# Attention of a hybrid decoder layer: queries' low parts by one full-height subtraction and two copies, outputs' low parts by an adding DMA, one masked product for two halves

## The chip, the cores and the metric

The kernel runs on one core of a Trainium2 chip. The metric is the device time of one execution in microseconds. Before the change the median of three runs was 1638.94 us, the runs lying between 1638.71 and 1641.65 us. The core has engines that each run their own list of instructions in order: TensorE (PE: matmuls into PSUM banks), VectorE (DVE), ScalarE (ACT), GpSimd (POOL) and SyncE (SP). GpSimd and SyncE are used here mostly to issue DMAs.

## The reference

One inference step of one layer, for a prompt of 1024 positions and 8 x 8 sample positions (1088 columns in all) with a width of 1024:

```python
xn = rmsnorm(x, norm1_g)
q, k, v, glu_a, glu_b, gate_a, gate_b = split(xn @ w_in)
# branch A: sliding-window attention, window 128, 16 query heads on 4 key/value heads, head width 64
s = q @ k.T * HEAD_DIM ** -0.5, masked to the band, one learned sink per head appended
attn = softmax(s)[..., :-1] @ v
branch_a = attn @ w_o_attn
# branch B: gated causal depthwise convolution (31 taps), LayerNorm, silu
u = glu_a * sigmoid(glu_b)
branch_b = silu(layernorm(dwconv(u))) @ w_pb
h = x + (sigmoid(gate_a) * branch_a + sigmoid(gate_b) * branch_b) @ w_out
# feed-forward with a causal depthwise convolution of 3 taps
y = h + (silu(gate) * value) @ w_down, gate and value from dwconv(rmsnorm(h) @ w_up)
```

Everything is float32; both groups get a final RMSNorm, and windows of keys, values and convolution inputs are returned too.

## The kernel before

**Products in three parts.** Each float32 operand is kept as a high part, rounded to the matmul's reduced float32 type, and a low part, which is the rest. `mm3` (L208 to L210) makes one product of three matmuls: high by high, high by low, low by high. A "stream" (`stream`, L212) takes one 1024 x 128 block of an input weight over the three chunks of columns, 384, 384 and 320 wide, with eight `mm3` each, and hands each finished PSUM bank to an evacuation routine. For most blocks of the input weight the high part is a cast on ScalarE (L179), the low part begins as its negative (ScalarE, L180), and GpSimd's DMA adds the raw weight to it (L181, `wlo<-wraw`). Raw weights come by SP (L157, `wraw<-wall`), into two buffers in turn.

**The order of the streams** is written out by hand: `b a g g g q0 q0 b a q0 q0 k0 b a v v`, `g b a g b a g g g b a`, `q1 k1 q1 q1 q1 b a g b a g g g g g g g`. Here b and a are the two halves of the gated unit of one channel block, g a gate, q0 and q1 the query blocks of the two halves of the heads, k0 and k1 their keys, v the values. After `v`, and again after the last `q1`, attention for one half (`p` = 0, then 1) is spread over the streams that follow by a count of ticks, one for each `mm3`: eight units (`attn_unit`, one for each block of 128 positions) and four sample units. A unit has for each of two key heads `g` three steps: `scores` (L440, matmuls L449 and L450), `turn` (L457, transposes and the split of the probabilities into `pth` and `ptl`), and `mix` (L476, products with the values).

**What the change touches.** `q_evac` (L815) evacuates the queries. The query tile `q0` holds for key head 0 the high part in partitions 0 to 63 and the low part in 64 to 127, and `q1` the other way round. For each chunk and each of the two tiles, ScalarE scales 64 rows into the high place (L823), and VectorE subtracts it from the bank into the low place (L824). In `turn`, two products with a band mask (L471) make the parts that belong to the block below. In `mix`, the summed result `av` is split into `q0` and `q1` at the places of the queries it came from (`split_ps`: ScalarE's cast L243, VectorE's subtraction L244). For the first half, `attn_spill` (L502) stores both parts to `d_ah` and `d_al` after blocks 3 and 7; the output projection's `o` streams load them much later (`ah`, `al`).

**The convolution** of a channel block (`conv`, L570) runs on VectorE, as some 45 multiply-adds (L582) at a low priority, so that they fill VectorE between other work. It ends with L601 to L604, and GpSimd stores the result (L605, L606, `d_c<-u`). `u` has two buffers; the next but one block's start (`u_start`, L748) loads history columns into it by SP (L752, `u<-cbT`), which must wait for that store. When all eight are stored, the LayerNorm over channels starts (`ln_steps`, L608): SP loads the results back (L634, `ct<-d_c`), VectorE adds them up (L620), and TensorE forms the mean (L628), which stands at a fixed place among the matmuls.

A scheduler fixes each engine's order of instructions when the program is built, by priorities and its own estimate of readiness; on the chip each engine then keeps to that order.

Of the kernel before, what the change touches and what calls it, by code (L numbers as in the profile page):

```python
# [6 lines left out]
F32 = mybir.dt.float32  # L7
F32R = mybir.dt.float32r
AF = mybir.ActivationFunctionType
# [120 lines left out]
class Build:  # L130
# [291 lines left out]
    def attn_unit(self, p, blk, st):  # L422
# [34 lines left out]
        def turn(g):  # L457
# [4 lines left out]
            ph = self.t(self.at, [P, 512], "pth", F32R)  # L462
            pl = self.t(self.at, [P, 512], "ptl", F32R)
            parts = [(0, ph), (0, pl)]
            with self.later(TURN_SOONER if self.now - self.gated <= 3 else 0):
                self.split_ps(ph, pl, ps)
                if blk:
                    below = self.masks[:, None, WIN:2 * WIN].to_broadcast([P, 4, WIN])
                    for x, tag in ((ph, "pth0"), (pl, "ptl0")):
                        x0 = self.t(self.at, [P, 512], tag, F32R)  # L470
                        nc.vector.tensor_tensor(x0.rearrange("p (a b) -> p a b", a=4),  # L471
                                                x.bitcast(F32).rearrange("p (a b) -> p a b", a=4), below, ALU.mult)
                        parts.append((1, x0))
            live[g]["parts"] = parts

        def mix(g):  # L476
# [6 lines left out]
            if g == 0:  # L483
                live[0]["t"] = self.t(self.at, [P, 4 * P], "av").rearrange("p (a b) -> p a b", a=4)
# [4 lines left out]
            if g == 1:  # L489
                self.split_ps(q[0][:, :, qs], q[1][:, :, qs], t)  # L490
            if p == 0 and g == 1 and blk in (3, 7):
                b0 = (blk - 3) * P
                self.attn_spill(st, slice(b0, b0 + 4 * P))
# [14 lines left out]
    def sample_unit(self, p, bp, st):  # L508
# [19 lines left out]
        def turn():  # L528
# [4 lines left out]
            ts = live["ts"] = self.t(self.at, [P, 4 * P], "av")[:, 0:2 * P]  # L533
# [196 lines left out]
    def phase_x(self):  # L730
# [60 lines left out]
        def do_a(i, u):  # L791
            self.stream(("a", i), xs, a_evac(u))
            a_done(i, u)
# [21 lines left out]
        def q_evac(p, j):  # L815
            st = q_tiles(p)

            def ev(c, o, n, ps):
                m = min(n, SEQ - o)
                for g in range(2):  # L820
                    r, x = [slice(y * HD, (y + 1) * HD) for y in (g, 1 - g)]
                    q = st["q"][g][:, j, o:o + m]
                    nc.scalar.activation(q[r], ps[r, :m], AF.Identity, scale=HD ** -0.5)  # L823
                    nc.vector.scalar_tensor_tensor(q[x], ps[r, :m], HD ** -0.5, q[r].bitcast(F32),  # L824
                                                   ALU.mult, ALU.subtract)
# [1398 lines left out]
```

## Time and profile before

| | |
|---|---|
| median of 3 runs | 1638.94 us |
| profiled execution | 1639.45 us |
| span of its instructions | 1637.7 us |
| TensorE's mean granted clock | 0.998 |
| TensorE waits named by the trace, longest first | 4.7 us (two), 2.0, 1.1, 0.6 us |

A line of a group reads: source line, engine, operation, output<-inputs, shape, number of instructions, then busy time in us and mean ns of one, then the idle time ahead of them and what ended it. A line of a timeline reads: start, duration in us, engine, line, operation, tiles, and in brackets the idle time before and what ended it; "SPq" and "POOL ... DMA" rows are the issue of a transfer, not the transfer. A line of a window reads: from and to, its length, then busy time and number of instructions on PE, PE's weight loads, DVE, ACT and POOL, the granted clock, the mean busy share of the 16 DMA engines, and GB/s. A line of DMA issues ends with the KB of one and the median us from issue to landing.

### The profile page before, as it was taken

To read this page: it belongs to the slowest core of one execution; us is meant where nothing else is said; L and a number is where in the kernel's file an instruction comes from. 1 tells how busy PE (TensorE), PEld (TensorE's weight loads), DVE (VectorE), ACT (ScalarE), POOL (GpSimd) and SP (SyncE) were. 2 spreads that over 40 slices of the span, in tenths; PEclk is the share of its full clock that TensorE was granted. 3 is DMA by queue.
4 is the path that set the end of the run, shared out by engine and by line. 5 is a ranking of instruction groups with operands and counts; after the bars stand their busy time and mean duration, and the time that the engine had idled before them with its cause. 6 is when DMAs were issued, how large, how long until landed. Compare 5 with 4: busy or idle time off the path is not lost.

```text
span 1637.7 us, 30023 instructions
## 1 busy us (share of the span) xinstructions
PE 1621.8 (99%) x11428; PEld 1602.6 (98%) x11428; DVE 1369.8 (84%) x2463; ACT 901.9 (55%) x1948; POOL 301.6 (18%) x587
## 2 busy tenths in 40 slices
PE   9999999999999999999999999999999999999998
PEld 9999999999999999999999999999999999999998
DVE  7889678999869996788755999988888877889767
ACT  6535387875588754576532465555555555524322
POOL 0210122333112221111102422322222111000000
PEclk9999999999999999999999999999999999999999
DMA  6343433545433366548763632344444334676423
GB/s 211 98 98 90 114 95 97 140 132 143 109 85 78 118 215 202 176 154 232 188 227 102 209 119 72 112 116 118 119 120 109 106 106 157 225 177 160 110 62 110
DMA packets 110329, 221.51 MB, mean 135 GB/s; under 512 B 26600, under 2 KB 57320, under 8 KB 110168
## 3 DMA queue, kind: packets, MB, share of 16 engines
q1 hardware_dynamic: 81528, 131.47, 26.0%
q0 software_dynamic: 28224, 87.71, 20.2%
q8 instruction: 90, 1.47, 0.4%
q14 instruction: 55, 0.45, 0.1%
q10 hardware_dynamic: 432, 0.40, 0.1%
HBM read 137.55 MB, written 64.03 MB: 123 GB/s over the span
## 4 chain that ended last, share of the span: by engine, by line
PE 80%; DVE 8%; DMA 4%; issue 4%; ACT 3%; POOL 0%; SPq 0%; POOLq 0%; DVEq 0%; ACTq 0%
PE mm L208 19%; PE mm L209 19%; PE mm L210 19%; PE aux L210 6%; PE aux L208 6%; PE aux L209 6%; DVE c L582 2%; PE aux L482 1%; DVE bt L582 1%; DVE q L824 1%; PE aux L461 1%; PE aux L449 1%; PE aux L450 1%; DMA ct<-d_c 1%; DMA wlo<-wraw 1%
## 5 line engine op out<-in xcount | busy, mean ns | idle before, releaser
L208 PE MATMUL mm<-xh,whi 128*128 128x384 f32 (+1 forms) x904 | 299.2, 331 | 0.2 <-ACT xh L297 0.2
L209 PE MATMUL mm<-xl,whi 128*128 128x384 f32 (+1 forms) x904 | 296.4, 328 | 0.4 <-DVE xl L298 0.4
L210 PE MATMUL mm<-xh,wlo 128*128 128x384 f32 (+1 forms) x904 | 296.3, 328 | 0.3 <-DMA wlo<-wraw 0.3
L209 PEld LDWEIGHTS mm<-xl,whi 128*128 128x128 f32 x904 | 170.5, 189 | 2.5 <-DVE xl L298 0.9
L208 PEld LDWEIGHTS mm<-xh,whi 128*128 128x128 f32 x904 | 170.5, 189 | 2.0 <-ACT xh L297 0.7
L210 PEld LDWEIGHTS mm<-xh,wlo 128*128 128x128 f32 x904 | 170.2, 188 | 1.1 <-DMA wlo<-wraw 0.7
L1470 DVE SCALAR_TENSOR_TENSOR acc<-st,fc,acc 128x1104 f32<-128x1104 f32 x88 | 119.8, 1364 | 12.2 <-issue 6.7
L582 DVE SCALAR_TENSOR_TENSOR bt<-u,consts,bt 128x513 f32<-128x513 f32 x120 | 89.6, 746 | 3.7 <-ACT bt L592 3.1
L210 PE MATMUL mm<-th,wlo 128*128 128x272 f32 x320 | 92.3, 289 | 0.0
L209 PE MATMUL mm<-tl,wlo 128*128 128x272 f32 x320 | 92.3, 288 | 0.0
L208 PE MATMUL mm<-th,wlo 128*128 128x272 f32 x320 | 92.2, 288 | 0.0
L582 DVE SCALAR_TENSOR_TENSOR c<-sm,hsum,c 128x512 f32<-128x512 f32 x120 | 89.3, 745 | 0.5
L210 PE MATMUL mm<-mh,wlo 128*128 128x272 f32 (+4 forms) x304 | 88.9, 292 | 0.0
L582 DVE SCALAR_TENSOR_TENSOR c<-u,consts,c 128x512 f32<-128x512 f32 x112 | 83.4, 744 | 0.4
L243 ACT CAST whi<-wraw 128x512 fp32r<-128x512 f32 x76 | 47.5, 625 | 62.7 <-PE aux L210 25.7
L1815 ACT COPY st<-mm 128x272 f32<-128x272 f32 (+2 forms) x132 | 43.5, 348 | 54.0 <-PE mm L210 53.8
L243 ACT CAST wlo<-wraw 128x512 fp32r<-128x512 f32 x76 | 47.3, 623 | 40.1 <-DVE wraw L1666 16.6
L1468 ACT ACTIVATE acc<-st,fc 128x1104 f32<-128x1104 f32 x44 | 57.6, 1315 | 14.9 <-DVE st L1771 11.8
L208 PE MATMUL aux<-mh,whi 128*128 128x272 f32 (+4 forms) x216 | 63.8, 295 | 0.0
L209 PE MATMUL aux<-ml,whi 128*128 128x272 f32 (+4 forms) x216 | 63.5, 294 | 0.0
L244 DVE TENSOR_TENSOR wlo<-wraw,wlo 128x512 fp32r<-128x512 f32 x76 | 52.7, 695 | 9.5 <-ACT wlo L243 9.3
L208 PEld LDWEIGHTS mm<-th,wlo 128*128 128x128 f32 x320 | 60.2, 188 | 0.0
(726 smaller groups left out, 5799.2 us busy)
## 6 DMA issues: line engine op xcount, KB each, us to landing
wraw<-wall SPq DMA_DIRECT2D x118, 512.0 KB, 3.8
wlo<-wraw POOLq DMA_DIRECT2D x37, 512.0 KB, 4.5
bw<-d_b SPq DMA_DIRECT2D x42, 272.0 KB, 3.9
d_b<-gd POOLq DMA_DIRECT2D x36, 272.0 KB, 6.1
d_b<-acc POOLq DMA_DIRECT2D x24, 272.0 KB, 4.7
ar<-wdn SPq DMA_DIRECT2D x32, 192.0 KB, 3.8
d_g<-acc POOLq DMA_DIRECT2D x10, 544.0 KB, 4.7
ga<-d_ga SPq DMA_DIRECT2D x8, 544.0 KB, 5.4
```

Of the source, the lines that this page charges most:

```text
L208: mm(ps, wh, xh, start=first, stop=False, skip_group_check=more)
L209: mm(ps, wh, xl, start=False, stop=False, skip_group_check=more)
L210: self.last_mm = mm(ps, wl, xh, start=False, stop=last, skip_group_check=more).ins
L243: self.cast = self.nc.scalar.copy(h, src).ins
L244: self.low = self.nc.vector.tensor_tensor(l, src, h.bitcast(F32), ALU.subtract).ins
L449: nc.tensor.matmul(ps[:, j, :], q[g][:, h, qs], kd[g][:, keys], start=True, stop=False)
L450: nc.tensor.matmul(ps[:, j, :], q[g][:, h, qs], kl[g][:, keys], start=False, stop=True)
L461: nc.tensor.transpose(ps[:, h * P:(h + 1) * P], pt[:, h, 0:P], self.ident)
L582: mac = lambda o, x, w: nc.vector.scalar_tensor_tensor(o, x, w, o, ALU.mult, ALU.add)
L1468: nc.scalar.activation(acc, st[:, 0:AW], AF.Identity, bias=fb(f), scale=fw(f, 0))
L1470: nc.vector.scalar_tensor_tensor(acc, st[:, k:k + AW], fw(f, k), acc, ALU.mult, ALU.add)
L1815: self.evicted = (add if second and n == 0 and j == 1 else op)(d, r(banks[bank, j]))
```

## The change

`q_evac` scales all 128 rows into `q0` (ScalarE), subtracts all 128 rows into a new tile `ql` with two buffers (VectorE, one instruction), scales 64 rows into `q1`, and SP copies the two halves of `ql` to their places. `turn` keeps the two parts in one tile and masks them with one product of 1024 columns. `mix` has two buffers for `av`; the low part of the output begins as the negative of the high part (ScalarE) and GpSimd's DMA adds `av` to it. The first spill moves from block 3 to block 4, and `do_a` asks for one more split weight where a value stream comes next.

```diff
@@ turn
-            ph = self.t(self.at, [P, 512], "pth", F32R)
-            pl = self.t(self.at, [P, 512], "ptl", F32R)
-            parts = [(0, ph), (0, pl)]
+            x = self.t(self.at, [P, 2, 512], "pt", F32R)
+            parts = [(0, x[:, y]) for y in range(2)]
...
-                    below = self.masks[:, None, WIN:2 * WIN].to_broadcast([P, 4, WIN])
-                    for x, tag in ((ph, "pth0"), (pl, "ptl0")):
-                        x0 = self.t(self.at, [P, 512], tag, F32R)
-                        nc.vector.tensor_tensor(x0.rearrange("p (a b) -> p a b", a=4),
-                                                x.bitcast(F32).rearrange("p (a b) -> p a b", a=4), below, ALU.mult)
-                        parts.append((1, x0))
+                    below = self.masks[:, None, WIN:2 * WIN].to_broadcast([P, 8, WIN])
+                    x0 = self.t(self.at, [P, 2, 512], "pt0", F32R)
+                    nc.vector.tensor_tensor(x0.rearrange("p y (a b) -> p (y a) b", a=4),
+                                            x.bitcast(F32).rearrange("p y (a b) -> p (y a) b", a=4), below, ALU.mult)
+                    parts += [(1, x0[:, y]) for y in range(2)]
@@ mix
-                live[0]["t"] = self.t(self.at, [P, 4 * P], "av").rearrange("p (a b) -> p a b", a=4)
+                live[0]["t"] = self.t(self.at, [P, 4 * P], "av", bufs=2).rearrange("p (a b) -> p a b", a=4)
...
-                self.split_ps(q[0][:, :, qs], q[1][:, :, qs], t)
-            if p == 0 and g == 1 and blk in (3, 7):
-                b0 = (blk - 3) * P
+                h, l = q[0][:, :, qs], q[1][:, :, qs]
+                nc.scalar.copy(h, t)
+                nc.scalar.activation(l, h.bitcast(F32), AF.Identity, scale=-1.0)
+                nc.gpsimd.dma_start(l, t, accum_op=ALU.add)
+            if p == 0 and g == 1 and blk in (4, 7):
+                b0 = blk // 7 * 4 * P
@@ do_a
-            self.stream(("a", i), xs, a_evac(u))
+            self.stream(("a", i), xs, a_evac(u), ahead=1 + (self.order[self.w_used + 1][0] == "v"))
@@ q_evac
-                for g in range(2):
-                    r, x = [slice(y * HD, (y + 1) * HD) for y in (g, 1 - g)]
-                    q = st["q"][g][:, j, o:o + m]
-                    nc.scalar.activation(q[r], ps[r, :m], AF.Identity, scale=HD ** -0.5)
-                    nc.vector.scalar_tensor_tensor(q[x], ps[r, :m], HD ** -0.5, q[r].bitcast(F32),
-                                                   ALU.mult, ALU.subtract)
+                q0, q1 = [q[:, j, o:o + m] for q in st["q"]]
+                low = self.t(self.at, [P, 384], "ql", F32R, bufs=2)[:, :m]
+                nc.scalar.activation(q0, ps[:, :m], AF.Identity, scale=HD ** -0.5)
+                nc.vector.scalar_tensor_tensor(low, ps[:, :m], HD ** -0.5, q0.bitcast(F32), ALU.mult,
+                                               ALU.subtract)
+                nc.scalar.activation(q1[HD:], ps[HD:, :m], AF.Identity, scale=HD ** -0.5)
+                nc.sync.dma_start(q0[HD:].bitcast(F32), low[:HD].bitcast(F32))
+                nc.sync.dma_start(q1[:HD].bitcast(F32), low[HD:].bitcast(F32))
```

Lines behind these places carry numbers that are one to three higher in the changed kernel.

The change moves instructions at three places that matter below. The first is VectorE at the last chunks of the last `q1` stream, ahead of the first scores of the second half. The `c`, `bt` and `u` rows are a convolution and its end. Before:

```order
L824 SCALAR_TENSOR_TENSOR q_508_4287<-mm_4702,q_508_4287 64x384
L582 SCALAR_TENSOR_TENSOR c_4226<-sm_4227,hsum_87,c_4226 128x512
L824 SCALAR_TENSOR_TENSOR q_509_4288<-mm_4702,q_509_4288 64x384
L601 TENSOR_SCALAR u_3956<-c_4226,consts_77 128x64
L602 TENSOR_TENSOR c_4226<-c_4226,bt_4228 128x512
L604 TENSOR_TENSOR u_3956<-c_4226,bt_4228 128x512
L603 TENSOR_TENSOR u_3956<-c_4226 128x512
L824 SCALAR_TENSOR_TENSOR q_508_4287<-mm_4731,q_508_4287 64x384
L824 SCALAR_TENSOR_TENSOR q_509_4288<-mm_4731,q_509_4288 64x384
L824 SCALAR_TENSOR_TENSOR q_508_4287<-mm_4760,q_508_4287 64x256
L824 SCALAR_TENSOR_TENSOR q_509_4288<-mm_4760,q_509_4288 64x256
```

Now:

```order
L583 SCALAR_TENSOR_TENSOR c_4214<-sm_4215,hsum_87,c_4214 128x512
L602 TENSOR_SCALAR u_3949<-c_4214,consts_77 128x64
L603 TENSOR_TENSOR c_4214<-c_4214,bt_4216 128x512
L605 TENSOR_TENSOR u_3949<-c_4214,bt_4216 128x512
L824 SCALAR_TENSOR_TENSOR ql_4662<-mm_4637,q_490_4275 128x384
L604 TENSOR_TENSOR u_3949<-c_4214 128x512
L824 SCALAR_TENSOR_TENSOR ql_4693<-mm_4668,q_490_4275 128x256
L824 SCALAR_TENSOR_TENSOR ql_4733<-mm_4708,q_490_4275 128x384
L824 SCALAR_TENSOR_TENSOR ql_4764<-mm_4739,q_490_4275 128x384
L824 SCALAR_TENSOR_TENSOR ql_4795<-mm_4770,q_490_4275 128x256
```

The convolution's end stood behind the first chunk of the last query block (two subtractions); now it stands behind the middle chunk of the block before it, four subtractions of the old kind sooner, and one subtraction to `ql` takes the place of two.

The second is SP's queue at the same place, which had no query copies; before it read:

```order
L157 DMA wraw_541_4695<-wall 128x1024
L157 DMA wraw_548_4795<-wall 128x1024
L752 DMA u_643_5426<-cbT 128x8x30
L157 DMA wraw_568_4951<-wall 128x1024
L157 DMA wraw_613_5237<-wall 128x1024
```

Now, with the copies of the last two query blocks:

```order
L827 DMA q0_490_4275<-ql_529_4662 64x384
L828 DMA q1_491_4276<-ql_529_4662 64x384
L827 DMA q0_490_4275<-ql_531_4693 64x256
L828 DMA q1_491_4276<-ql_531_4693 64x256
L753 DMA u_629_5429<-cbT 128x8x30
L827 DMA q0_490_4275<-ql_536_4733 64x384
L828 DMA q1_491_4276<-ql_536_4733 64x384
L157 DMA wraw_542_4807<-wall 128x1024
L827 DMA q0_490_4275<-ql_538_4764 64x384
L828 DMA q1_491_4276<-ql_538_4764 64x384
L827 DMA q0_490_4275<-ql_540_4795 64x256
L828 DMA q1_491_4276<-ql_540_4795 64x256
```

The history load `u<-cbT`, which waits for the convolution's store, stood among weight loads; now six copies of the last query block stand behind it.

The third is GpSimd's queue at the last block of the first half's attention: the spill (`d_ah`, `d_al`; eight issues, of which the first row here is the seventh) and a weight's adding DMA (`wlo`). Before:

```order
L505 DMA d_ah_1_57<-q0_27_123 128x512
L506 DMA d_al_2_58<-q1_28_124 128x512
L517 DMA vp_603_5132<-vp 128x2x128
L393 COPY sp_605_5140<-nsrow_19_88 128x1
L181 DMA wlo1_500_4125<-wraw_471_3960 128x1024
```

Now, with the adding DMA of the last block's output, `q1<-av`, among them:

```order
L813 MEMSET qs_492_4277 128x768
L393 COPY sp_593_5145<-nsrow_19_88 128x1
L506 DMA d_ah_1_57<-q0_27_123 128x512
L491 DMA q1_28_124<-av_468_4004 128x4x128
L506 DMA d_ah_1_57<-q0_27_123 128x512 x3
L507 DMA d_al_2_58<-q1_28_124 128x512 x4
L181 DMA wlo1_482_4113<-wraw_457_3953 128x1024
```

The load of `vp` now stands behind the weight's adding DMA and the small copy `sp` ahead of the spill; the adding DMA of the output stands inside the spill, whose later rows read what it writes, and all of it ahead of the weight's.

More of the change, by code (lines that the diff above doesn't have):

```diff
@@ L532, in turn @@
             nc.tensor.transpose(tr[:, P:2 * P], pt[:, 0, 64:192], self.ident)
-            ts = live["ts"] = self.t(self.at, [P, 4 * P], "av")[:, 0:2 * P]
+            ts = live["ts"] = self.t(self.at, [P, 4 * P], "av", bufs=2)[:, 0:2 * P]
             nc.scalar.copy(ts, tr[:, 0:2 * P])
```

2 lines of the change are left out of this document (1 added, 1 removed).

## The prediction

> **What bounds the kernel now.** I read the page's busy line first, then TensorE's waits (us in total, times, longest), then TensorE's timeline and windows around each.
>
> ```profile
> PE 1621.8 (99%) x11428; PEld 1602.6 (98%) x11428; DVE 1369.8 (84%) x2463; ACT 901.9 (55%) x1948; POOL 301.6 (18%) x587
> PE aux L628 <- DVE sm L620: 4.7, 2, 3.4
> PE mm L209 <- DMA wlo<-wraw: 2.0, 1, 2.0
> PE mm L714 <- DVE least L708: 1.1, 1, 1.1
> ```
>
> TensorE is busy for 1621.8 of 1637.7 us. The change removes none of its matmuls, so all it can win is TensorE's idle time, some 16 us by the busy line, and what a halved clock costs after an idle stretch. Nearly all that the waits name lies in four places: 4.7 us in two waits of the LayerNorm mean (L628), 2.0 us for one low weight part, 0.58 us at an attention score (next fence), and 1.1 us at L714, which is at the start of the program and untouched. So the question is not how much VectorE saves in all, but what stands behind three of these waits. The places:
>
> ```profile
> 177.99 0.28 PE L208 MATMUL mm<-whi,xh 128*128 128x256 f32 x1
> 180.31 0.39 PE L209 MATMUL mm<-wlo,xh 128*128 128x256 f32 x1 [2.04 <-DMA wlo<-wraw]
> ...
> 460.37 0.39 PE L449 MATMUL aux<-kd,q 128*128 128x256 f32 x1 [0.58 <-DVE ptl L244]
> ...
> 629.05 1.24 PE L628 MATMUL aux<-sm,mean 128*128 128x272 f32 x2 [3.36 <-DVE sm L620]
> ...
> 692.90 0.72 PE L628 MATMUL aux<-sm,mean 128*128 128x272 f32 x2 [1.37 <-DVE sm L620]
> ```
>
> The third costs more than its 3.36 us:
>
> ```profile
> 628.00:630.00 2.00, 0.95 (x3) 0.84 (x3) 1.49 (x4) 0.48 (x1) 0.75 (x2) 0.76 1.15 345
> 630.00:632.00 2.00, 2.00 (x9) 1.91 (x8) 1.42 (x4) 0.00 (x0) 0.17 (x1) 0.50 0.94 373
> 632.00:634.00 2.00, 2.00 (x14) 2.00 (x14) 2.00 (x1) 0.00 (x0) 0.00 (x0) 0.88 0.05 20
> ```
>
> The third column from the end is the granted clock: 0.76, 0.50, 0.88. The shares lost, 0.24, 0.50 and 0.12 of 2 us each, make 1.7 us. The wait of 2.04 us left the clock at 1.00 (its window, 175 to 200 us, shows 1.00). A page of the Trainium skill, "TensorE: Matmul & The Clock Gate", says under "Part 1: The HAM clock gate" that the clock halves after about one idle window of 3.4 us. The trace agrees at this one place: 3.36 us idle, then half speed; by that rule any shorter wait left here would give back the 1.7 us as well.
>
> **The change part by part.** First the prices on VectorE, ScalarE and the queues.
>
> ```profile
> L824 DVE SCALAR_TENSOR_TENSOR q<-mm,q 64x384 fp32r<-64x384 f32 x32 | 17.8, 555 | 1.6 <-ACT q L823 0.6
> L824 DVE SCALAR_TENSOR_TENSOR q<-mm,q 64x256 fp32r<-64x256 f32 x16 | 6.8, 422 | 2.3 <-ACT q L823 1.9
> L244 DVE TENSOR_TENSOR aw<-ar,aw 128x384 fp32r<-128x384 f32 x24 | 13.3, 554 | 2.0 <-ACT aw L243 1.4
> L471 DVE TENSOR_TENSOR ptl<-ptl,masks 128x512 fp32r<-128x512 f32 x28 | 19.1, 683 | 0.0
> L1480 DVE TENSOR_TENSOR acc<-acc,acc 128x1024 f32<-128x1024 f32 x22 | 26.8, 1217 | 0.0
> L244 DVE TENSOR_TENSOR q<-av,q 128x512 fp32r<-128x512 f32 x16 | 11.0, 686 | 1.9 <-ACT q L243 1.8
> L243 ACT CAST q<-av 128x512 fp32r<-128x512 f32 x16 | 9.8, 613 | 1.0 <-DVE av L488 1.0
> L180 ACT ACTIVATE wlo<-whi 128x1024 fp32r<-128x1024 f32 x37 | 39.1, 1057 | 0.2
> wlo<-wraw POOLq DMA_DIRECT2D x37, 512.0 KB, 4.5
> d_c<-u POOLq DMA_DIRECT2D x8, 512.0 KB, 2.9
> d_ga<-gt POOLq DMA_DIRECT2D x16, 192.0 KB, 2.2
> ```
>
> - Queries: a 128x384 subtraction takes 554 ns and a 64x384 one 555, so rows are free. 48 subtractions become 24: VectorE saves 16 x 0.555 + 8 x 0.422 = 12.3 us. ScalarE keeps its number of instructions. SP issues 48 more copies of up to 96 KB. No row shows such a copy. Its landing is bounded below by 0 and above by the 2.2 us of a 192 KB store; I take 2.2, the nearest row.
> - Masks: 56 products of 0.683 become 28 of 1024 columns. The nearest row, L1480, has 1217 ns, so VectorE saves 28 x (1.366 - 1.217) = 4.2 us.
> - Attention outputs: 16 subtractions of 0.686 go, 11.0 us of VectorE. ScalarE gets 16 more activations of 512 columns; the bounds are 0.613 (the cast of that size) and 1.057 (L180, twice as wide), I take 0.613, so 9.8 us. GpSimd gets 16 adding DMAs of 256 KB, which should land in 2.2 to 4.5 us by the 192 KB and 512 KB rows; I take the middle, 3.4. Their result is read only by a spill to memory and by the output projection, far later.
>
> Together VectorE loses some 27 us of its 1369.8. What is it worth at each place?
>
> **Place A, 180 us.** The low weight part that TensorE waits for comes out of a long chain in order on ScalarE, behind the evacuation of the first keys.
>
> ```profile
> 123.68 0.55 DVE L824 SCALAR_TENSOR_TENSOR q<-mm,q 64x384 fp32r<-64x384 f32 x1
> ...
> 147.31 0.43 DVE L824 SCALAR_TENSOR_TENSOR q<-mm,q 64x256 fp32r<-64x256 f32 x1
> ...
> 155.74 0.47 ACT L849 CAST kd<-mm 64x384 fp32r<-64x384 f32 x1 [1.18 <-DVE kl L848]
> 157.24 1.05 ACT L179 CAST whi<-wraw 128x1024 fp32r<-128x1024 f32 x1
> 169.24 1.05 ACT L179 CAST p<-wraw 128x1024 fp32r<-128x1024 f32 x1 [5.29 <-DMA wraw<-wall]
> 175.08 0.87 POOL L181 DMA_DIRECT2D wlo<-wraw  x1 [2.35 <-ACT wlo L180]
> ```
>
> Read backwards: the adding DMA at 175.08 follows casts that waited for a raw load (169.24), which waited for the slot of the weight cast at 157.24, which stood behind a key copy that waited for VectorE's L848. VectorE worked without a break there. Between 123.68 and 147.31 it ran 12 of the query subtractions, 8 wide and 4 narrow. Six of them go: 4 x 0.555 + 2 x 0.422 = 3.1 us. The chain moves up by as much, the DMA to 172.0, its landing from 180.3 to about 177.2, and it is wanted 0.15 us after 177.99. The wait goes: **-2.0 us**. Bounds: 0 if the keys then wait for TensorE instead, -2.04 in full.
>
> **Place B, 460 us.** ScalarE and VectorE alternate on the chunks of the last query group until the row below, though TensorE began the scores of the second half at 440.50 (quoted further down); from there ScalarE has no gap up to the cast that leads to the score at 460.37.
>
> ```profile
> 445.70 0.42 DVE L824 SCALAR_TENSOR_TENSOR q<-mm,q 64x256 fp32r<-64x256 f32 x1 [0.94 <-ACT q L823]
> ```
>
> A shorter evacuation brings all of it forward: **-0.6**. Bounds: 0 and -0.6, and the new cost below.
>
> **Place C, 629 us.** This is the largest piece. It starts at the end of the last convolution.
>
> ```profile
> 612.94 0.68 DVE L603 TENSOR_TENSOR u<-c 128x512 f32<-128x512 f32 x1
> 613.92 0.54 POOL L605 DMA_DIRECT2D d_c<-u  x1 [1.26 <-DVE u L603]
> 616.75 0.33 SPq L157 DMA_DIRECT2D wraw<-wall  x1
> 620.37 2.28 SPq L634 DMA_DIRECT2D ct<-d_c  x3
> 475.00:600.00 125.00, 125.00 (x792) 120.91 (x791) 121.65 (x238) 97.76 (x278) 26.91 (x48) 1.00 0.40 109
> 608.00:620.00 12.00, 12.00 (x75) 12.00 (x74) 5.62 (x10) 2.88 (x3) 2.51 (x4) 1.00 1.04 368
> 620.00:622.00 2.00, 2.00 (x13) 2.00 (x12) 0.00 (x0) 1.93 (x3) 0.16 (x1) 1.00 0.25 67
> ```
>
> VectorE is full from 475 to 600 us (121.65 of 125), with the second half's attention ahead of the convolutions. There it saves 8 x 0.686 for the outputs and 14 x 0.149 for the masks, 7.6 us, so the convolution ends near 606 instead of 613.6. But TensorE will not get 7.6 us: the reload of the result (L634) stands on SP behind a weight load issued at 616.75, so it can rise from 620.37 to about 617.1 at most. And the DMA engines are full until 620 (share 1.04) and slack only from 620 to 622 (0.25): 1.5 us of work fits there. So the reload ends between 1.5 and 3.3 us earlier. I take 2.2, nearer to the bandwidth's end. The wait shrinks from 3.36 to 1.2: **-2.2**, and with a wait of 1.2 us, below the 2.04 that left the clock alone, the halved clock goes: **-1.7**.
>
> The fourth place (692.90) hangs on TensorE's own progress, so I leave it: 0, bounds -1.4 and +1.5 (the size of that wait, either way).
>
> **New costs.** ScalarE's activations add 8 x 0.613 = 4.9 us to the 97.76 of 125 us between 475 and 600, where TensorE does not wait at all now; the spare time covers them, and if it didn't, TensorE would wait for as much. On SP a new hazard stands ahead of the first scores of the second half.
>
> ```profile
> 441.05 0.68 DVE L603 TENSOR_TENSOR u<-c 128x512 f32<-128x512 f32 x1
> ...
> 445.16 0.55 SPq L752 DMA_DIRECT2D u<-cbT  x1
> ...
> 440.50 0.28 PE L449 MATMUL aux<-kd,q 128*128 128x256 f32 x1
> ```
>
> The copies of the last query group stand behind the history load (u<-cbT), which waits until the previous convolution has been stored. That convolution ended at 441.73. Four query subtractions that ran ahead of its end now stand behind it (2 x 0.555 + 2 x 0.422 = 2.0 us), and the eight chunks before it have one subtraction instead of two (8 x 0.51 = 4.1 us): it ends at 435.6 at the latest, and up to 7.6 us sooner if what VectorE saves in the first half's attention (8 x 0.686 + 14 x 0.149) carries over. From its end to the copies' landing I count 0.54 (issue of the store) + 2.9 + 0.55 + 2 x 0.4 + 2.2 = 7.0 us. That gives 435.0 to 442.6, against 440.50: TensorE waits for between 0 and 2.1 us. The middle, 438.8, is in time; I take **+0.5** for the later part of that stretch.
>
> On GpSimd the adding DMA of the first half's last block, and the spill that reads it, stand ahead of a weight's adding DMA; the spill must wait for the landing taken above, so that weight can come between 0 and 3.4 us later. Against that, two small steps that it stood behind now stand elsewhere, and the spill's eight DMAs stood ahead of it before too. I take 0 and keep 3.4 as an end. The first spill comes one block later and no longer reads a fresh result; its reader is the output projection, much later: 0. A second buffer for the outputs can only take waits away: 0. The edit of `do_a` has a weight split asked for one stream sooner ahead of the first value stream; on ScalarE the two casts of place A keep their order, so 0, bounds 0 and the 2.0 us of A.
>
> A rule speaks against these copies: "DMA: Bandwidth & Descriptors" in the Trainium skill, under "Rules for kernel authors", advises against two transfers to disjoint partition halves, because they serialize. No run here shows such a pair; by it the second copy lands one transfer later, at most another 2.2 us in the estimate above.
>
> **The sum:** -2.0 - 0.6 - 2.2 - 1.7 + 0.5 = -6.0 us against the profiled 1639.45 us, so 1633.45. The median, 1638.94, is 0.5 us below the profiled execution; I give the same step from there: **1633 us**. With every term at its favourable end (C -3.3, fourth place -1.4, no new wait) it is -9.0, 1630.
>
> **The rivals.**
> - *The wait at 629 stays.* The reload is bound by the DMA engines and by SP's order, not by VectorE; a residue of some 3 us keeps the half clock. For it: the share of 1.04 until 620. Against it: the 1.5 us of slack after it. Then only A and B and the +0.5 count: -2.1, so about 1636.8, within 0.2%.
> - *Nothing is won.* VectorE's time is filled with convolution anyway, and the key evacuation at 155 us is set by TensorE. Then about 1639. Against it: VectorE is without a gap ahead of both places.
> - *A new wait outweighs all.* The history load on SP blocks the copies. If the convolution ended as late as now, 441.7, the copies would land at 448.7 and TensorE would stand still for 8.2 us at 440.5, with 1.7 us of half clock behind it: +9.9, against A, C and the clock's -5.9 a net +4, 1643. It decides from a convolution end of about 433.5, and the whole is slower by more than 0.2% if it ends after 441.
> - *More is won*: the wait at 629 goes in full and the one at 693 with it, 1630.
>
> **How the numbers follow.** Forecast with its terms within a microsecond or two: 0.60. Wait at 629 stays: 0.17. Nothing won: 0.08. New wait outweighs: 0.10. More won: 0.05. A measurement of this kernel tells some 0.2%, 3.3 us, from no change, so faster begins below 1635.7. The forecast's upper edge, with the full wait of 2.1 us at 440 (1634.6), is still faster; 0.03 of its chance, with two terms short at once, is not. So faster 0.57 + 0.05 = 0.62, same 0.03 + 0.17 + 0.07 = 0.27, slower 0.10 + 0.01 = 0.11. The range, from 1629.5 to 1638, leaves out the slower rival and most of the one without a gain.
>
> **What would show it.** Right: no wait of L209 for wlo<-wraw near 178; none of L449 for ptl near 458; L628's first wait near 623 below 2 us, with a granted clock of 1.00 behind it; the last d_c<-u issued some 7 us earlier against TensorE's work; no new row in TensorE's waits above 1 us. Wrong: a wait of L449 for DMA q<-ql near 438; L628 still waiting for over 3 us with 0.50 behind it; waits for ScalarE between 470 and 600; VectorE's busy time down by much less than 27 us.

## The result and the profile after

The changed kernel takes 1645.17 us (median of 7 runs, 1643.63 to 1646.45), the kernel before 1638.94 beside it (7 runs): ratio 1.0034, with a 95% interval from 1.0022 to 1.0046. It is **slower by about 0.34%**. The forecast was 1633 us with a range up to 1638.0, so the time lies outside it, on the other side of no change. The profiled execution of the changed kernel is the fastest of the seven, 1643.63 us, with a span of 1641.9 against 1637.7. The two traces below differ by 4.2 us; by the ratio the medians differ by some 5.6, and no trace shows the rest.

The first fence has the busy line of the changed kernel's page; the second its TensorE waits (total, times, longest, in us).

```profile
PE 1624.3 (99%) x11428; PEld 1604.0 (98%) x11428; DVE 1344.5 (82%) x2395; ACT 912.2 (56%) x1964; POOL 329.0 (20%) x603
```

```profile
PE aux L629 <- DVE sm L621: 6.0, 2, 4.7
PE mm L210 <- DMA wlo<-wraw: 1.8, 1, 1.8
PE mm L209 <- DMA wlo<-wraw: 1.3, 1, 1.3
```

VectorE lost 1369.8 - 1344.5 = 25.3 us of work, as meant. TensorE nevertheless waits longer: the mean (L629, formerly L628) waited 4.7 us in all and now 6.0, and a wait of 1.8 us for a weight is new. The score's wait is gone, and that for the first weight has shrunk from 2.0 to 1.3. Where that happens is read by following the same instruction in both traces. TensorE's timeline, changed kernel:

```profile
179.50 0.39 PE L209 MATMUL mm<-wlo,xh 128*128 128x256 f32 x1 [1.27 <-DMA wlo<-wraw]
...
382.17 0.34 PE L209 MATMUL mm<-xl,whi 128*128 128x384 f32 x1
384.33 0.51 PE L210 MATMUL mm<-xh,wlo 128*128 128x384 f32 x1 [1.82 <-DMA wlo<-wraw]
...
444.92 0.28 PE L449 MATMUL aux<-kd,q 128*128 128x256 f32 x1
...
629.29 0.34 PE L210 MATMUL mm<-xh,wlo 128*128 128x384 f32 x1
634.35 1.25 PE L629 MATMUL aux<-sm,mean 128*128 128x272 f32 x2 [4.72 <-DVE sm L621]
...
697.92 0.73 PE L629 MATMUL aux<-sm,mean 128*128 128x272 f32 x2 [1.32 <-DVE sm L621]
```

And those of the same instructions in the kernel before that were not shown above:

```profile
381.37 0.34 PE L209 MATMUL mm<-xl,whi 128*128 128x384 f32 x1
381.55 0.35 PE L210 MATMUL mm<-xh,wlo 128*128 128x384 f32 x1
...
625.35 0.34 PE L210 MATMUL mm<-xh,wlo 128*128 128x384 f32 x1
```

| TensorE's instruction | before | after | later by |
|---|---|---|---|
| behind the first weight's wait | 180.31 | 179.50 | -0.8 |
| in front of the new wait | 381.37 | 382.17 | +0.8 |
| behind the new wait | 381.55 | 384.33 | +2.8 |
| first scores of the second half | 440.50 | 444.92 | +4.4 |
| in front of the mean | 625.35 | 629.29 | +3.9 |
| the mean | 629.05 | 634.35 | +5.3 |
| second mean | 692.90 | 697.92 | +5.0 |
| span | 1637.7 | 1641.9 | +4.2 |

Four pieces make it slower: +1.6 over the first half's attention (from 180 to 381 us, in no named wait), +2.0 at the new wait (1.82 of it the wait), another +1.6 behind that wait, and +1.4 at the mean. Against them stand 0.8 at the first weight's wait, 0.5 (440 to 625) where the score's wait has gone, 0.3 between the means and some 0.8 at the end. The +1.6 behind the wait is the clock. The windows of the changed kernel, granted clock third from the end:

```profile
383.00:385.00 2.00, 0.67 (x3) 0.67 (x4) 2.00 (x7) 1.97 (x4) 0.00 (x0) 0.89 0.49 108
385.00:387.00 2.00, 2.00 (x8) 2.00 (x7) 1.78 (x3) 0.02 (x1) 1.99 (x4) 0.50 0.82 233
387.00:389.00 2.00, 2.00 (x11) 2.00 (x10) 0.00 (x0) 0.00 (x0) 2.00 (x4) 0.76 0.63 131
```

The shares lost (0.11, 0.50, 0.24 of 2 us each) make 1.7 us, although the wait was only 1.82.

**Where the wait at 384 comes from.** The weight's adding DMA left GpSimd late. GpSimd's timeline, changed kernel; the number in brackets is the idle time before a row and what ended it:

```profile
370.08 0.55 POOL L506 DMA_DIRECT2D d_ah<-q  x1 [0.58 <-ACT u L765]
371.09 1.33 POOL L491 DMA_DIRECT2D q<-av  x1 [0.46 <-ACT u L765]
371.87 2.20 POOL L506 DMA_DIRECT2D d_ah<-q  x3
375.98 2.13 POOL L507 DMA_DIRECT2D d_al<-q  x4 [1.90 <-DMA q<-av]
378.10 0.91 POOL L181 DMA_DIRECT2D wlo<-wraw  x1
```

Before:

```profile
374.20 0.92 POOL L181 DMA_DIRECT2D wlo<-wraw  x1 [0.34 <-issue]
```

The weight's DMA comes 3.9 us later. It stands behind the spill, and the spill's second half (`d_al`) reads what the adding DMA writes, so GpSimd waits 1.90 us for its landing. But that isn't all: the adding DMA itself is issued late, because the output it needs is late. ScalarE's copy of the last block's second product, before:

```profile
362.85 0.58 ACT L487 COPY av<-aux 64x512 f32<-64x512 f32 x1 [1.93 <-PE aux L482]
```

ScalarE, changed kernel:

```profile
362.79 0.59 ACT L243 CAST pt<-aux 128x512 fp32r<-128x512 f32 x1 [2.48 <-DVE pt L469]
...
367.31 0.58 ACT L485 COPY av<-aux 64x512 f32<-64x512 f32 x1 [0.21 <-PE aux L480]
```

That copy is 4.5 us later. The joined tile `pt` has one buffer for both key heads; ScalarE's cast for the second head waits for VectorE's joined product (L469) of the first, which reads both halves. In TensorE's fixed order, the last value product of the first half has accordingly moved from behind 1907 to behind 1931 of the three-part matmuls, and it starts 4.4 us later (366.87 instead of 362.42).

**Why the mean waits longer.** The store of the last convolution is issued, and SP reloads the result, at (GpSimd first, then SP's queue, changed kernel):

```profile
613.28 0.55 POOL L606 DMA_DIRECT2D d_c<-u  x1 [0.18 <-issue]
```

```profile
623.55 1.93 SPq L635 DMA_DIRECT2D ct<-d_c  x2
```

The store leaves at 613.28, against 613.92 before: with TensorE 3.9 us later, that is 4.6 us earlier against TensorE's work. But from store to reload it is now 10.3 us, where it was 6.4, so the reload gained only 0.8. A window of the changed kernel, DMA share and GB/s last:

```profile
620.00:624.00 4.00, 4.00 (x26) 4.00 (x25) 0.00 (x0) 0.74 (x1) 0.00 (x0) 1.00 1.02 416
```

The DMA engines are full here too, with 416 GB/s; the slack that stood from 620 to 622 us (a share of 0.25) is gone. Most of the bytes in flight should be the loads of the spilled outputs (`ah` and `al`, 4.4 MB, issued from 600 us back), which an experiment below moves. Then VectorE's sums, changed kernel:

```profile
630.18 0.30 DVE L621 TENSOR_TENSOR sm<-u 128x136 f32<-128x136 f32 x1
630.48 1.23 DVE L190 TENSOR_TENSOR wlo<-wraw,whi 128x1024 fp32r<-128x1024 f32 x1
631.62 0.72 DVE L621 TENSOR_TENSOR u<-ct 128x544 f32<-128x544 f32 x1
...
633.27 0.73 DVE L621 TENSOR_TENSOR u<-ct 128x544 f32<-128x544 f32 x1 [0.45 <-DMA ct<-d_c]
633.91 0.29 DVE L621 TENSOR_TENSOR sm<-u 128x136 f32<-128x136 f32 x1
```

The mean needs the two rows `sm`. Between them now stand a weight's split (L190), which was ahead of the first sum before, and an addition of the next LayerNorm unit, which even waits for its reload.

### The profile page after: what moved, and what is told of

Same layout as the page of the kernel before. It is cut to its first block, busy times and chain, and to the rows that moved or that the text cites. A ratio compares the mean times of both kernels' runs of the same rounds, so it can differ in the third digit from the quotient of the medians.

```text
span 1641.9 us, 30127 instructions
## 1 busy us (share of the span) xinstructions
PE 1624.3 (99%) x11428; PEld 1604.0 (98%) x11428; DVE 1344.5 (82%) x2395; ACT 912.2 (56%) x1964; POOL 329.0 (20%) x603
## 4 chain that ended last, share of the span: by engine, by line
PE 89%; DMA 4%; ACT 3%; DVE 2%; issue 2%; POOL 0%; SPq 0%; POOLq 0%; DVEq 0%; ACTq 0%
PE mm L210 21%; PE mm L209 21%; PE mm L208 21%; PE aux L210 7%; PE aux L209 7%; PE aux L208 7%; PE aux L480 2%; DMA wlo<-wraw 1%; PE aux L461 1%; PE aux L449 1%; PE aux L450 1%; DMA ct<-d_c 1%; DMA d_c<-u 1%; ACT p L416 1%; PE aux L522 0%
## 5 line engine op out<-in xcount | busy, mean ns | idle before, releaser
L179 ACT CAST whi<-wraw 128x1024 fp32r<-128x1024 f32 x37 | 38.9, 1052 | 42.9 <-PE mm L209 34.1
```

The costliest lines, as they stand in the source:

```text
L179: self.cast = self.nc.scalar.copy(h, r).ins
```

## The experiments

The **theory** from these rows: the join makes the last value product late, and the spill, waiting for the adding DMA, hands this on to the weight; either of the two alone would make no wait there. The mean's growth comes with the adding DMAs alone (order of sums, queue of DMAs). The **rival** (D below) is that the 48 new copies load the DMA engines and delay both the weight and the reload. Ratios are to the kernel before in runs on the same chip, with 95% intervals. First, each part of the change is undone or done alone.

**Without the join** (two tiles, as before, all else changed):

```diff
-            x = self.t(self.at, [P, 2, 512], "pt", F32R)
+            ph = self.t(self.at, [P, 512], "pth", F32R)
+            pl = self.t(self.at, [P, 512], "ptl", F32R)
...
-                    below = self.masks[:, None, WIN:2 * WIN].to_broadcast([P, 8, WIN])
+                    below = self.masks[:, None, WIN:2 * WIN].to_broadcast([P, 4, WIN])
...
```

> The changed kernel with two masked products of 512 columns and separate tiles for the high and low parts, as before. Theory S (the spill): joining the parts in one tile moves the last product with the values of the first half from behind 1907 to behind 1931 of the three-part matmuls, so the output, its adding DMA, the spill and then the weight's adding DMA on GpSimd come late; without the join the wait of L210 for wlo near 384 (1.8 us) and the halved clock behind it go: about 3.5 us faster than the changed kernel, 1641.7 us; the wait at the LayerNorm mean stays at 4.7. Theory D (the DMA engines are loaded by the new copies and adding DMAs): no difference, 1645. Theory A (ScalarE's 16 more activations): no difference, 1645.

1640.17 us, ratio 1.0004 (0.9994 to 1.0013). Its GpSimd timeline:

```profile
371.29 2.16 POOL L509 DMA_DIRECT2D d_al<-q  x4 [2.55 <-DMA q<-av]
...
374.15 0.95 POOL L181 DMA_DIRECT2D wlo<-wraw  x1
```

GpSimd waits for the adding DMA here even longer (2.55), but 4.7 us sooner: the weight's DMA leaves at 374.15, and the wait at 384 is gone. Of its waits of TensorE:

```profile
PE aux L631 <- DVE sm L623: 5.4, 2, 4.6
```

The mean's wait stays, so it does not need the join. TensorE's instruction in front of the place, at 382.17 in the changed kernel, stands at 380.70: the +1.6 over the first half's attention belongs to the join too.

**Without the adding DMAs:**

```diff
-                h, l = q[0][:, :, qs], q[1][:, :, qs]
-                nc.scalar.copy(h, t)
-                nc.scalar.activation(l, h.bitcast(F32), AF.Identity, scale=-1.0)
-                nc.gpsimd.dma_start(l, t, accum_op=ALU.add)
+                self.split_ps(q[0][:, :, qs], q[1][:, :, qs], t)
```

> The changed kernel with the outputs split as before by a cast and a VectorE subtraction. Theory S: the spill no longer waits for an adding DMA (1.9 us), so the wait for wlo near 384 falls below 0.5 us; the sums ahead of the first LayerNorm mean stand in the old order on VectorE again, so that wait falls from 4.7 to about 3.4: about 4.5 us faster than the changed kernel, 1640.5 us. Theory D: the adding DMAs were the load, 1640 or less and the convolution's store lands sooner than 10 us after its issue. Theory A: the small waits for ScalarE's L420 between 275 and 375 go, 1 us, 1644.

1639.66 us, 1.0001 (0.9993 to 1.0010). ScalarE's last copy of the value product is late here too (367.83; the product stands behind 1923 of the three-part matmuls), and yet there is no such wait at 384: without the adding DMA the late product makes none. The sums stand in their old order, and the mean waits 2.0 us at the longest, 4.1 in three pieces. This run does not part S from D: D's forecast came true as well (below 1640 us, and 7.8 us from store to reload instead of 10.3). Below, the last block's output alone does so for the wait at 384, and the moved loads for the mean.

**Without the query copies:**

```diff
-                q0, q1 = [q[:, j, o:o + m] for q in st["q"]]
...
-                nc.sync.dma_start(q1[:HD].bitcast(F32), low[HD:].bitcast(F32))
+                for g in range(2):
...
+                    nc.vector.scalar_tensor_tensor(q[x], ps[r, :m], HD ** -0.5, q[r].bitcast(F32),
+                                                   ALU.mult, ALU.subtract)
```

> The changed kernel with the queries evacuated as before (no copies on SP). Theory S: both new losses stay, and the old waits of 2.0 us near 180 and 0.6 us near 460 come back: 1646 to 1647 us. Theory D: 48 transfers fewer, so 2 us faster than the changed kernel, 1643. Theory A: no difference from S.

1644.49 us, 1.0031 (1.0020 to 1.0043). TensorE's waits:

```profile
PE aux L629 <- DVE sm L621: 5.4, 3, 4.5
PE mm L209 <- DMA wlo<-wraw: 2.2, 1, 2.2
PE mm L210 <- DMA wlo<-wraw: 1.8, 1, 1.8
```

Both new waits (1.8 and 4.5) are there without a single copy, so the copies do not make them: D falls for the copies. S missed too, with a time above the measured one: the wait near 180 is back, but the score's wait is not, though the queries are evacuated as before.

**The queries' part alone** (the kernel before with the new `q_evac`):

> The kernel before with the queries' part of the change alone. Theory S: the wait near 180 shrinks from 2.0 to 1.3 us and the one near 460 goes, nothing is added: 1637.5 us, 1.4 faster than before. Theory D: SP's copies delay loads, 1640 or more.

1638.37 us, 0.9990 (0.9982 to 0.9999). The score's wait is gone, the first weight's is 1.6, the mean's 3.8. This part helps a little at most (the interval ends just below 1), and nothing shows a cost of its copies.

Then the wait at 384 from its two ends, with the rest of the change kept. **A second buffer for the joined tile:**

```diff
-            x = self.t(self.at, [P, 2, 512], "pt", F32R)
+            x = self.t(self.at, [P, 2, 512], "pt", F32R, bufs=2)
```

> The changed kernel with two buffers for the joined tile of the two parts (pt). Theory S (the joined tile is freed only when the joined product has read both halves, so the next turn's cast waits): the last product with the values of the first half stands behind 1922 of the three-part matmuls instead of 1931, 1.6 us earlier; the wait for wlo near 384 falls from 1.8 to about 0.2 us and the halved clock behind it goes: ratio to the kernel before 1.0015 instead of 1.0034. Rival (the product of 1024 columns is itself too long): no difference, 1.0034.

1641.93 us, 1.0015 (1.0006 to 1.0024). The last value product stands behind 1922 of the matmuls instead of 1931, the wait is 0.7 us, and no half clock follows. TensorE's instruction in front of the place stands at 380.86 instead of 382.17, so most of the +1.6 goes with the single buffer. But the mean's wait, which the expectation left out, fell too:

```profile
PE aux L629 <- DVE sm L621: 4.4, 2, 3.4
```

VectorE's sums stand in the changed kernel's order here, but the first addition starts 1.6 us before TensorE gets to the mean (624.55 against 626.18), where in the changed kernel it was 0.7 (628.95 against 629.63). So the time came out as expected partly for another reason, and the mean's wait hangs on when the reload lands as well as on the order of the sums.

**The last block's output by VectorE's subtraction**, so that the spill waits for no DMA there:

```diff
-                nc.scalar.activation(l, h.bitcast(F32), AF.Identity, scale=-1.0)
-                nc.gpsimd.dma_start(l, t, accum_op=ALU.add)
+                if p == 0 and blk == 7:
+                    nc.vector.tensor_tensor(l, t, h.bitcast(F32), ALU.subtract)
+                else:
+                    nc.scalar.activation(l, h.bitcast(F32), AF.Identity, scale=-1.0)
+                    nc.gpsimd.dma_start(l, t, accum_op=ALU.add)
```

> The changed kernel with the low part of one output, that of the first half's last block, subtracted on VectorE instead of added by a DMA. Theory S: TensorE's order stays as in the changed kernel, the spill's later issues no longer wait 1.9 us for the adding DMA's landing, so the weight's adding DMA goes out about 1.9 us sooner and the wait of L210 near 384 falls from 1.8 to below 0.3 us, with no halved clock behind it; the LayerNorm wait stays at 4.5: ratio to the kernel before 1.0015 to 1.002. Rival (the late place of the last product alone makes the wait): it stays above 1.2 us, ratio 1.003.

1641.64 us, 1.0022 (1.0012 to 1.0032); its interval overlaps that of the whole change, so the size of the gain rests on the trace. There TensorE's order is that of the changed kernel, the product as late, and GpSimd's row reads:

```profile
376.63 0.91 POOL L181 DMA_DIRECT2D wlo<-wraw  x1 [0.69 <-ACT q L243]
```

This is 1.5 us sooner than 378.10, although TensorE is 1.6 us later in this execution (383.74 in front of the place instead of 382.17), and the wait at 384 is gone. Without the join, or without the adding DMA of this one block, there is no wait; both are shown to be needed for it.

Next, the mean. **The sums in their old order** (the next unit's sums only behind the last of the first):

```diff
+            with ExitStack() as es:
+                if i == 1:
+                    es.enter_context(self.tc.issue_after(self.summed))
-            for y, r in enumerate(each(ct)):
-                reduce(y, r, self.t(self.cv, [P, 4, n], "u", bufs=2))
+                for y, r in enumerate(each(ct)):
+                    reduce(y, r, self.t(self.cv, [P, 4, n], "u", bufs=2))
```

> The changed kernel with the sums of the second LayerNorm unit issued behind the last sum of the first. If the third addition, which waits for its reload in front of the last sum, costs what the trace of the changed kernel shows (VectorE idle 0.45 us and 0.73 us of addition less their overlap, about 1.1 us): the wait at the first mean falls from 4.7 to about 3.6 us, ratio to the kernel before 1.0025 to 1.003. If only the landing of the reloads counts: no difference, 4.5 to 4.8 us, 1.0034.

1642.38 us, 1.0023 (1.0014 to 1.0032), an interval that overlaps that of the whole change. The mean's wait falls from 4.7 to 3.4, what it was before the change; the weight's split still stands between the sums. So the foreign addition and its wait for the reload are enough to make the growth of 1.3 us, and the gain that was forecast is missing besides. The growth can go in another way too: with two buffers for the joined tile it went with the addition still in its place. The wait at 384 (1.88 us here) is untouched.

**The loads of the spilled outputs behind the first reload:**

```diff
-                nc.sync.dma_start(r, self.d_c[:, :, x * n:x * n + n].rearrange("k p t -> p k t"))
+                last = nc.sync.dma_start(r, self.d_c[:, :, x * n:x * n + n].rearrange("k p t -> p k t")).ins
+            if i == 0:
+                with self.tc.issue_after(last):
+                    self.parts()
...
-                for (o, w) in CHUNKS:
+                def parts():
+                    for (o, w) in CHUNKS:
...
+                self.parts = parts
```

> The changed kernel with the six loads of the first half's attention (ah, al) issued on SP behind the first reload of the convolution (ct) instead of at the start of the last four gate streams. Theory D2 (the convolution ends earlier, but its store and reload wait in the DMA engines behind 4.4 MB of those loads): the store lands 3 us after its issue instead of 10, the reload about 6 us sooner, the wait at the first LayerNorm mean falls from 4.7 to below 1 us and the halved clock goes: 5 to 6 us faster than the changed kernel, ratio 1.000. Rival O (the order of the sums on VectorE and of SP's queue sets it): the wait stays above 3 us.

1640.40 us, 1.0008 (0.9998 to 1.0019). The store was issued at 611.31; SP's queue:

```profile
616.04 1.01 SPq L635 DMA_DIRECT2D ct<-d_c  x2
```

So the reload follows the store after 4.7 us instead of 10.3, and the first mean no longer waits. The gain is less than the 5 to 6 us expected, since another mean waits 2.8 us in its place, at 639.8, where the second reload has now come to stand behind the 4.4 MB. The wait at 384 (1.84) stays, as it should.

**The same edit without the change:**

> The kernel before with the same late loads alone. Theory D2: the wait at the mean falls from 3.4 to below 1 us though the convolution ends as late as it did, and the halved clock goes: ratio 0.997. Rival C (the convolution's end sets the wait, as the prediction had it): the wait stays near 3 us, ratio 1.000.

1634.91 us, 0.9975 (0.9965 to 0.9986). Its waits of TensorE, and SP's queue:

```profile
PE aux L628 <- DVE sm L620: 1.8, 2, 1.3
PE mm L209 <- DMA wlo<-wraw: 1.3, 1, 1.3
```

```profile
616.96 1.00 SPq L634 DMA_DIRECT2D ct<-d_c  x2
```

The mean waits 1.3 us with VectorE as busy as before (the reload rises from 620.37 to 616.96). So 2.1 of the 3.4 us hung on the queue of DMAs and not on VectorE. The 1.3 that is left is more than the 1 expected; in the run before, where the convolution ends sooner, it is gone at this mean.

**Both together without the join:**

> The changed kernel without the joined product and with the late loads. If S and D2 add up: no wait for wlo near 384, none above 1 us at the mean, the wait near 180 at 1.3 us: ratio 0.9965. If VectorE's savings count for nothing once the loads are out of the way: the same as the kernel before with late loads alone, 0.997.

1633.95 us, 0.9968 (0.9955 to 0.9980). The time is as expected, but one mean waits 2.1 us (at 658.59), where none above 1 was expected, and the interval overlaps that of late loads alone: that VectorE's savings count for something here is not shown.

**The same, with the loads split** (one chunk behind the first reload, two behind the second):

```diff
-            if i == 0:
+            if i < 2:
                 with self.tc.issue_after(last):
-                    self.parts()
+                    self.parts(CHUNKS[1:] if i else CHUNKS[:1])
...
```

> The changed kernel without the joined product and with the loads of ah and al split: the first chunk behind the first reload of the convolution, the others behind the second. If the wait of 2.1 us at 658 (and the halved clock behind it) in the run with all loads between the reloads comes from the second reload being behind 4.4 MB, it goes: 1.7 to 3.8 us faster than that run, ratio to the kernel before 0.9945 to 0.996. If it comes from VectorE's order, no difference: 0.997.

1634.89 us, 0.9976 (0.9967 to 0.9985). The gain that was expected did not come. The wait at 658 is gone, but the means still wait 3.4 us in three pieces, the longest 1.7, and a product now waits 0.5 us for the late loads. The bytes are only pushed about.

**The queries' part and the late loads, nothing else of the change:**

> The kernel before with the queries' part and the late loads. If the adding DMAs and ScalarE's activations bring nothing of their own: 0.997, as the changed kernel without the joined product with late loads (0.9968). If the earlier end of the convolution that they bring is worth something once the loads are out of the way: 0.9975.

1633.04 us, 0.9958 (0.9945 to 0.9972). The ratio is below both forecasts. This kernel beats the one before and the changed one and has the lowest ratio of those tried, but its interval overlaps those of the three before it. That the adding DMAs bring anything on top is not shown: with them the ratio was 0.9968 (the experiment before the last). Nor is it shown what the queries' part adds to the late loads.

## Why the prediction was wrong

- **The step that failed** is the one on GpSimd: "I take 0 and keep 3.4 as an end". It priced how long the spill might wait for the adding DMA's landing, and that was no bad guess (1.90 us). It left out that the output itself would come later. I had costed the join by VectorE's duration only, and did not ask when the joined tile comes free nor where TensorE's value product then stands. The two together made the weight's DMA 3.9 us late, for a wait of 1.82 and 1.7 of half clock, against 0 in the sum.
- **Place C failed too**: -2.2 and -1.7 were forecast, and it became +1.4, with the half clock kept. The convolution did end earlier against TensorE, by 4.6 of the 7.6 us. The step "the reload ends between 1.5 and 3.3 us earlier" did not hold: against TensorE the reload was issued only 0.8 us earlier. The step took a weight load on SP for what held the reload, and the slack of 620 to 622 us for room. What held it was the landing of the convolution's store: from store to reload the time grew from 6.4 to 10.3 us, and moving the other loads away cut it to 4.7. The order of the sums, worth up to 1.3, was not looked at. The rival "the wait at 629 stays" named the right cause at this place, at 0.17; it had no growth in it.
- **Place A held in its first link only**: -2.0 was forecast, -0.8 stands in this pair of traces, and not even that can be put down to the change. ScalarE's timeline, changed kernel:

```profile
154.63 1.06 ACT L179 CAST whi<-wraw 128x1024 fp32r<-128x1024 f32 x1
...
157.14 1.06 ACT L180 ACTIVATE wlo<-whi 128x1024 fp32r<-128x1024 f32 x1
...
168.21 1.05 ACT L179 CAST p<-wraw 128x1024 fp32r<-128x1024 f32 x1 [4.96 <-DMA wraw<-wall]
```

  The cast moved up by 2.6 us (157.24 before), near the 3.1 worked out. But the chain went on through the negative (L180), which now has more key copies between it and its cast, then through a raw load; the next cast moved only by 1.0 (169.24 before). And TensorE's wait goes with ScalarE's wait for that raw load, whichever kernel it is. In the six traces where ScalarE waits 4.93 to 5.01 us for it, TensorE waits 1.26 to 1.34; one of these is the kernel before with the late loads alone, which has the old evacuation (1.29). In the eight where ScalarE waits 5.29 to 5.60, TensorE waits 1.62 to 2.24, the two with the old evacuation the longest (2.04 and 2.24). So the shorter evacuation is worth between nothing and some 0.3 us here, an estimate from these groups. What makes the raw load take one time or the other is open.
- **Place B was right in its number**: the score's wait of 0.6 is gone, and the queries' part alone is enough for that. In the changed kernel it is gone without the new evacuation too (experiment without the query copies), so the shorter evacuation is not shown to be what removed it there. The hazard on SP, for which +0.5 was taken, did not come: the last convolution ended at 432.5, and the history load was issued at 436.34, before VectorE had even begun the first chunk of the last query block (437.98). That chunk's copies, issued at 438.56 and 439.08, landed by 442.7, ahead of the first scores at 444.92. The copies of the later chunks were issued up to 447.43, behind those scores, and TensorE has no named wait for them.
- **The prices on VectorE and ScalarE were right**; those of two transfers were too low. The groups of the changed kernel (lines first, then DMA issues with KB and median us):

```profile
L469 DVE TENSOR_TENSOR pt<-pt,masks 128x1024 fp32r<-128x1024 f32 x28 | 34.0, 1215 | 0.0
L490 ACT ACTIVATE q<-q 128x512 fp32r<-128x512 f32 x16 | 10.0, 626 | 0.1
```

```profile
q<-av POOLq DMA_DIRECT2D x16, 256.0 KB, 4.3
q<-ql SPq DMA_DIRECT2D x32, 96.0 KB, 3.1
```

  1.215 and 0.626 us were forecast as 1.217 and 0.613, but the adding DMA took 4.3 instead of 3.4, and a wide copy 3.1 instead of 2.2.
- **The slower rival** had the right sign with the wrong mechanism (copies behind the history load). That TensorE's own order could change was in no rival. The trace of before could not show it, but the instructions' order of both kernels, known ahead, could.

Open: which links of the first half's attention cost the 1.6 us between 180 and 381 (only that they go with the join, and mostly with its single buffer, is shown), what gave back some 0.8 us after the second mean, and why with two buffers for the joined tile TensorE is 4.9 us ahead of the changed kernel at the second mean (693.01 against 697.92) and only 1.5 at the end.

## What to carry to other kernels

Price an edit not only by the duration of its instructions but by when its tiles come free: joining two tiles makes the earlier part wait for the reader of both, and an order fixed ahead then moves other engines' work. A transfer that replaces arithmetic in an in-order queue turns each later reader in that queue into a wait for everything behind it. Where the last link of a wait is a DMA in full queues, freeing the engine ahead of it gives little (0.8 of 4.6 us here); moving bulk loads behind the urgent one gave 0.25% without touching any arithmetic. And before a shorter wait is credited to an edit, see whether it varies as much between executions that the edit does not touch.

## What the hardware showed

A wait well below the 3.36 us of before can halve TensorE's clock, and the same length need not. The changed kernel lost 1.7 us after 1.82 us at 384. Without the query copies, the same wait, on TensorE's timeline and in the windows behind it:

```profile
387.08 0.44 PE L210 MATMUL mm<-xh,wlo 128*128 128x384 f32 x1 [1.82 <-DMA wlo<-wraw]
```

```profile
385.00:387.00 2.00, 0.27 (x2) 0.00 (x0) 2.00 (x7) 1.97 (x3) 0.55 (x2) 1.00 0.87 173
387.00:389.00 2.00, 1.92 (x11) 1.92 (x12) 2.00 (x4) 0.79 (x2) 1.21 (x3) 1.00 0.49 81
```

The clock stays at 1.00. Without the adding DMAs, a wait near 180 us, and the windows:

```profile
180.59 0.39 PE L209 MATMUL mm<-wlo,xh 128*128 128x256 f32 x1 [1.89 <-DMA wlo<-wraw]
```

```profile
181.00:183.00 2.00, 2.00 (x13) 2.00 (x13) 0.00 (x0) 0.80 (x1) 0.15 (x1) 0.60 0.70 112
183.00:185.00 2.00, 2.00 (x12) 2.00 (x12) 1.05 (x2) 1.86 (x3) 0.00 (x0) 0.55 0.69 252
```

Here 1.89 us were followed by 0.60 and 0.55, while 2.04 us at the same matmul before the change were not. Of the seven traces that wait 1.85 to 2.24 us at this place, five show a half clock behind it. In the changed kernel with the late loads, even 2.81 us at 639.81 left the clock at 1.00. The Trainium skill, "TensorE: Matmul & The Clock Gate", "Part 1: The HAM clock gate", puts the fall at one or more idle windows of about 3.4 us; these rows disagree, since waits from 1.8 us on were enough at times. The same section says that the window runs freely, regardless of the kernel's start; that would fit a fall that depends on where in it a wait lies, though no run here shows the window itself. For a forecast it means that a wait of some 2 us costs 1.7 us more in some executions.
